# A decoder layer on one core: one comparison per group of tokens against numbers in PSUM, and the gates of a round loaded in quarters

## The chip, the core and the metric

The kernel runs on one core of one Trainium2 chip. The metric is the device time of the whole program in microseconds; the program is launched once per run. TensorE multiplies matrices, VectorE (DVE in the rows), ScalarE (ACT) and GpSimd (POOL) compute element by element, and SyncE (SP) issues most of the DMAs. VectorE and ScalarE read and write both on-chip memories, SBUF and PSUM; in this kernel every GpSimd operand lies in SBUF, and TensorE's results go to PSUM, in eight banks of 512 numbers per partition.

## The reference, cut to what matters

The layer has an input projection, a state-space scan, a windowed attention, an output projection with a layer norm, and then a feed-forward part with 128 x 128 = 16384 experts, of which each token uses 128 (8 heads with 16 each):

```python
e = (jnp.take_along_axis(i1, ci // PEER_TOPK, axis=-1) * PEER_NKEYS
     + jnp.take_along_axis(i2, ci % PEER_TOPK, axis=-1))
g = jax.nn.softmax(sc.astype(F32), axis=-1)
hid = jax.nn.gelu(jnp.einsum('thkd,td->thk', u_tab[e], xb).astype(F32), approximate=False)
return jnp.einsum('thk,thkd->td', (g * hid).astype(xb.dtype), v_tab[e])
```

An expert's number `e` is a row number (0 to 127, `e >> 7`) and a column number (0 to 127, `e & 127`). Only this part is touched by the change.

## The kernel before, in words

There are 1024 prompt tokens and 32 sample tokens. The first 448 prompt tokens have their experts' rows gathered one by one (`gathers`, from line 1808 on: GpSimd issues an indirect DMA for each, VectorE multiplies or accumulates, lines 1855 and 1860). The other 608 tokens go through all 16384 experts as dense products (`dense`, from line 1649 on): hidden values for all experts, times a gate that is zero for experts not chosen, times the second table. The two ways run at the same time: the gathers are a lane that is advanced by ticks between the products' matmuls, at a rate that spreads them over what is left.

**The table of gates.** Before the dense products can use them, the gates must be spread out: for each token a 128 x 128 table, row number by column number, that holds the gate where a chosen expert stands. `gates` builds it for 608 tokens in 152 groups of four. `experts` (line 1549) has put the row numbers (negated, line 1559), column numbers and gates of 128 tokens into a tile `eT` with the chosen experts on the partitions. `build` makes two tiles per group: `o2` (a comparison of 0 to 127 with the column number, line 1603 on VectorE, then times the gate, line 1604 on GpSimd) and `o1` (the same for the row number: on VectorE at line 1610 for three groups of five, on ScalarE at lines 1607 and 1608, as four Abs and one Relu, for two of five). `mults` (line 1617) multiplies them for each token on TensorE, `store` (line 1627) copies the result out of PSUM on ScalarE, and every eighth group goes to DRAM (`gd`, line 1629). `build` runs three groups ahead of `mults`; OBUFS = 4 buffers. One group is done in each tick.

The table is built beside the first six hidden products; `EARLY` gives their numbers of ticks, 8 to 40, so TensorE's order is a piece of a product, then a group's eight passes, and so on. All order is by hand: instructions stand in each engine's queue in the order in which the program issues them.

**The rounds.** The rest of `dense` runs over 16 rounds of eight rows of experts. A round has eight hidden products (Gelu at line 1673 on ScalarE, times the gates at line 1677 on VectorE, split into a high and a low part at lines 1680 and 1683) and eight output products (added to `r` at line 1701), the first two of which are one interleaved pair (`double`, line 1751). Each product is 48 matmuls (line 427). Its weights come in two loads of 256 KB (line 395, SyncE's queue), four products ahead, and are cast into a high part (line 368, ScalarE) and a low part (line 369, mostly GpSimd) two products ahead. Hidden products use three pairs of PSUM banks in turn. The gates of four rows are loaded by `table` (line 1663) as one DMA of 1216 KB from `gd` (line 1670), in pieces of 512 bytes; there are two buffers. The loop calls `table(q + 4)`: the load of a round's first four rows stands beside the fifth output product of the round before, that of the other four beside the round's first hidden product. Ends of groups of gathers (three of 128 tokens and one of 64) run a layer norm in `norm2`, which loads two rows of 512 KB (`lng`, line 1884), multiplies and adds on GpSimd (line 1885) and stores through SyncE's queue (line 1886).

Of the kernel before, what the change touches and what calls it, by code (L numbers as in the profile page):

```python
# [25 lines left out]
NE = 128  # L26
# [27 lines left out]
C_IOTE = C_TSEL + 16  # L54
C_NIOTE = C_IOTE + NE
C_PAY = C_NIOTE + NE
C_N = C_PAY + NPAIR

# [29 lines left out]

EQ, O1, OBUFS, EARLY = 4, "vavav", 4, [8, 16, 24, 30, 34, 40]


def const_arrays():
# [16 lines left out]
    c[:, C_IOTE:C_IOTE + NE] = np.arange(NE)[None, :]  # L109
    c[:, C_NIOTE:C_NIOTE + NE] = -np.arange(NE)[None, :]  # L110
    c[:, C_PAY:C_PAY + NPAIR] = (np.arange(NPAIR)[None, :] + 1) * PACK

# [139 lines left out]
class Build:  # L252
# [40 lines left out]
    def run(self):  # L293
# [10 lines left out]
        self.eps = cp.tile([128, 1], F32, name="eps")  # L304
        self.one = cp.tile([128, 1], F32, name="one")
        self.ctail = cp.tile([128, 20, 3], F32, name="ctail")
# [23 lines left out]
    def start(self):  # L330
        nc, t = self.nc, self.t
        load = [(self.cst, t["cst"]), (self.heads, t["heads"].unsqueeze(0).to_broadcast([128, 2, 24])),
                (self.convw, t["convw"]), (self.chans, t["chans"]), (self.keys, t["keys"])]
        self.xrp = self.open("xr", side="right")
        x = self.inputs(0)
        self.load(0, 0)
        next(x)
        self.load(0, 1)
        next(x)
        self.cast(0, 0)  # L340
        self.load(1, 0)
        next(x)
        self.cast(0, 1)
        self.load(1, 1)
        next(x)
        self.cast(1, 0)
        next(x)
        self.cast(1, 1)
        for _ in x:
            pass  # L350
        self.close("xr")
        for dst, src in load:
            nc.sync.dma_start(dst, src)
        nc.vector.memset(self.eps, EPS)
        nc.vector.memset(self.one, 1.0)
        nc.vector.memset(self.ctail, 0.0)
        nc.scalar.activation(self.heads[:, 1], self.heads[:, 1], AF.Exp)
        nc.vector.tensor_scalar_mul(self.heads[:, 1], self.heads[:, 1], -1.0)

        nc.vector.tensor_scalar_mul(self.convw, self.convw, 0.5)  # L360
        nc.vector.tensor_scalar_mul(self.chans[:, 12:24], self.chans[:, 12:24], 0.5)
# [1187 lines left out]
    def experts(self, sp, table, m, out):  # L1549
# [8 lines left out]
        nc.vector.tensor_copy(en[:m], ej[:m])  # L1558
        nc.vector.tensor_scalar_mul(en[:m, 0], en[:m, 0], -1.0)
        yield  # L1560
# [6 lines left out]
    def gates(self, sp):  # L1567
# [6 lines left out]
        groups = [(w, t) for w in range(len(work)) for t in range(work[w][2], work[w][2] + work[w][0], 4)]  # L1574
        eTs, o12, sts, outs, cp = dict(enumerate(self.given)), {}, {}, {}, {}

        def experts(w):
# [14 lines left out]
        def build(q):  # L1592
# [3 lines left out]
            eT = eTs[w]  # L1596
            o1 = sp.tile([128, 4, 128], F32, name="o1", tag="o1", bufs=OBUFS)
            o2 = sp.tile([128, 4, 128], F32, name="o2", tag="o2", bufs=OBUFS)

            def over(k):  # L1600
                return eT[:, k, t0:t0 + 4].unsqueeze(2).to_broadcast([128, 4, 128])

            nc.vector.tensor_tensor(o2, self.c(C_IOTE).unsqueeze(1).to_broadcast([128, 4, 128]), over(1), op=ALU.is_equal)  # L1603
            nc.gpsimd.tensor_tensor(o2, o2, over(2), op=ALU.mult)  # L1604
            if O1[q % len(O1)] == "a":
                for k in range(4):
                    nc.scalar.activation(o1[:, k], self.c(C_IOTE), AF.Abs, bias=eT[:, 0, t0 + k:t0 + k + 1])
                nc.scalar.activation(o1, o1, AF.Relu, scale=-1.0, bias=self.one)
            else:
                nc.vector.tensor_tensor(o1, self.c(C_NIOTE).unsqueeze(1).to_broadcast([128, 4, 128]), over(0), op=ALU.is_equal)  # L1610
            o12[q] = o1, o2

        def mults(q):
            o1, o2 = o12.pop(q)
            outs[q] = gp = self.bank(q % 3)
            for k in range(4):
                nc.tensor.matmul(gp[:, k * 128:(k + 1) * 128], o2[:, k], o1[:, k], start=True, stop=True)  # L1617

# [30 lines left out]
    def dense(self):  # L1649
# [12 lines left out]

        def table(q):
            if q >= len(steps):
                return
            c, half, k = steps[q]
            if not half and k % 4 == 0:
                gs[c, k // 4] = g = dp.tile([128, n // 32, 4, 32], F32, name="g", tag="g", bufs=2)
                e0 = c * 8 + k
                nc.sync.dma_start(g, self.gd[:, :, e0:e0 + 4, :].rearrange("b j i t -> j b i t"))  # L1670

# [95 lines left out]
        for k in range(8):  # L1767
            if k == len(EARLY):
                self.settle(table_lane)
                self.close("ga", "gc", "best")  # L1770
                dp = self.open("dn", 2)
                for q in range(8):
                    table(q)
            product(4 + k % 2 * 2, hs, EARLY[k] if k < len(EARLY) else DTICKS, lambda ps, k=k: early(k, ps))
# [6 lines left out]
        self.pumping.rate = self.left / ((len(steps) - 8) * DTICKS - 20)  # L1781
        for q in range(8, 12):
            table(q)
        for q, (c, half, k) in enumerate(steps[8:-LASTS], 8):
            table(q + 4)
            if half and k == 0:
# [118 lines left out]
```

## Time and profile before

| what | value |
|---|---|
| median of 3 runs | 3946.99 us (3944.28 to 3955.53) |
| the profiled execution | 3943.13 us, its span 3940.2 us |
| busy: TensorE | 3526.3 us, 89% |
| busy: VectorE | 2826.4 us, 72% |
| busy: GpSimd | 2494.5 us, 63% |
| busy: ScalarE | 1381.6 us, 35% |
| moved by DMA | 875.4 MB, mean 222 GB/s |
| granted clock of TensorE, mean | 0.945 |

How to read it: busy times are sums over the span, and stages with different limits are added up in them. The stretch in which the table of gates is built runs from about 1793 to 2172 us of the span, the rounds from there to about 3890. A line number in a row is that of the program; line 427 is where nearly all products are issued, lines 368, 369 and 395 belong to the weights. "xN" is a count, what stands in brackets or behind "<-" at the end of a row is what ended the idle time in front of it.

### The profile page before, as it was taken

The page shows a single profiled execution, that of the slowest core. Times are in us where ns is not written, and L with a number is a line of the kernel's source. Part 1 is how long each engine was busy: PE and PEld are TensorE (multiplying, and loading weights), DVE is VectorE, ACT ScalarE, POOL GpSimd, SP SyncE. Part 2 cuts the span into 40 slices and gives each one's busy share as a digit, 9 for nine tenths or more (in the row PEclk, how much of TensorE's full clock was granted, in tenths as well). Part 3 has the DMA queues.
Part 4 walks back from the last instruction along what each step waited for, and adds up shares of the span by engine and source line. Part 5 has one row for each costly group of instructions (what it writes and reads, how often), then busy time and mean ns, then how long its engine had stood idle before and what let it go on. Part 6 is the DMA issues. An engine that isn't in the chain of part 4 may idle for free.

```text
span 3940.2 us, 62009 instructions
## 1 busy us (share of the span) xinstructions
PE 3526.3 (89%) x22691; PEld 3178.6 (81%) x22691; DVE 2826.4 (72%) x5547; ACT 1381.6 (35%) x2651; POOL 2494.5 (63%) x2235
## 2 busy tenths in 40 slices
PE   7999898897997887895767999999999999999998
PEld 6757778895765555674666899999999999999997
DVE  2326644488779989899999767667766767776675
ACT  3423324343443333324778222222222222222223
POOL 3204554254747788645788677777767777776774
PEclk9999999998998998897778999999999999999999
DMA  5452235643546457522444789898988999998894
GB/s 159 127 164 74 75 128 199 211 156 107 155 158 212 152 161 249 195 73 78 158 158 185 258 314 324 314 339 316 335 309 318 327 319 339 329 324 304 309 320 154
DMA packets 385521, 875.40 MB, mean 222 GB/s; under 512 B 38976, under 2 KB 149952, under 8 KB 382272
## 3 DMA queue, kind: packets, MB, share of 16 engines
q0 software_dynamic: 129024, 469.82, 33.6%
q1 hardware_dynamic: 256192, 401.63, 30.6%
q8 instruction: 178, 2.92, 0.3%
q14 instruction: 127, 1.04, 0.1%
HBM read 805.40 MB, written 94.65 MB: 228 GB/s over the span
## 4 chain that ended last, share of the span: by engine, by line
PE 38%; DVE 12%; DMA 6%; issue 4%; POOL 3%; ACT 1%; SPq 0%; POOLq 0%; DVEq 0%; ACTq 0%
PE P L427 31%; PE P L1751 5%; DMA wraw<-in_ut 4%; DVE o L1603 2%; DVE acc L1860 2%; DVE o L1610 2%; POOL wlo L369 1%; POOL row L1829 1%; DVE row L1855 1%; POOL o L1604 1%; DMA lng<-in_ln 1%; PE P L1617 1%; DVE mr L1340 0%; PE P L1274 0%; DMA g<-gd 0%
## 5 line engine op out<-in xcount | busy, mean ns | idle before, releaser
L369 POOL TENSOR_TENSOR wlo<-wraw,whi 128x512 fp32r<-128x512 f32 (+1 forms) x621 | 818.2, 1324 | 652.7 <-ACT whi L368 620.5
L368 ACT ACTIVATE whi<-wraw 128x512 fp32r<-128x512 f32 (+1 forms) x820 | 494.8, 625 | 1318.2 <-PE P L427 485.9
L427 PE MATMUL P<-hh,whi 128*128 128x320 f32 (+3 forms) x2648 | 662.5, 315 | 35.9 <-DVE al L1683 27.4
L427 PE MATMUL P<-hh,wlo 128*128 128x320 f32 (+3 forms) x2648 | 655.9, 313 | 17.7 <-DVE wlo L369 9.5
L427 PE MATMUL P<-hl,whi 128*128 128x320 f32 (+3 forms) x2648 | 659.1, 313 | 3.5 <-POOL hl L1295 3.3
L1860 DVE SCALAR_TENSOR_TENSOR P<-row,hid,P 128x1024 f32<-128x1024 f32 x371 | 476.9, 1286 | 57.8 <-DMA row<-in_v,ecol 31.5
L1829 POOL DMA_INDIRECT row<-in_u,ecol x384 | 407.7, 1062 | 152.9 <-DVE row L1855 78.3
L427 PEld LDWEIGHTS P<-hh,whi 128*128 128x128 f32 x2648 | 452.2, 194 | 47.8 <-DVE al L1683 20.8
L427 PEld LDWEIGHTS P<-hh,wlo 128*128 128x128 f32 x2648 | 450.7, 193 | 28.0 <-DVE wlo L369 10.8
L1829 POOL DMA_INDIRECT row<-in_v,ecol x384 | 410.1, 1068 | 90.9 <-issue 71.5
L427 PE MATMUL P<-xh,whi 128*128 128x272 f32 (+4 forms) x1288 | 432.6, 346 | 32.9 <-ACT xh L368 17.3
L427 PEld LDWEIGHTS P<-hl,whi 128*128 128x128 f32 x2648 | 451.5, 193 | 12.8 <-POOL hl L1295 4.7
L1855 DVE SCALAR_TENSOR_TENSOR row<-row,P 128x1024 f32<-128x1024 f32 x320 | 381.8, 1215 | 102.6 <-DMA row<-in_u,ecol 74.0
L427 PE MATMUL P<-xl,whi 128*128 128x272 f32 (+4 forms) x1288 | 420.8, 337 | 7.6 <-POOL xl L369 6.6
L427 PE MATMUL P<-xh,wlo 128*128 128x272 f32 (+4 forms) x1288 | 418.0, 335 | 1.7 <-POOL wlo L369 1.7
L369 DVE TENSOR_TENSOR wlo<-wraw,whi 128x512 fp32r<-128x512 f32 (+1 forms) x199 | 222.7, 1119 | 212.4 <-ACT whi L368 188.3
L427 PE MATMUL P<-ah,wlo 128*128 128x320 f32 (+1 forms) x1536 | 341.9, 302 | 3.1 <-POOL wlo L369 3.1
L427 PE MATMUL P<-ah,whi 128*128 128x320 f32 (+1 forms) x1536 | 342.9, 302 | 0.0
L427 PE MATMUL P<-al,whi 128*128 128x320 f32 (+1 forms) x1536 | 341.4, 301 | 0.0
L1617 PE MATMUL P<-o,o 128*128 128x128 f32 x1216 | 219.2, 338 | 117.1 <-POOL o L1604 99.1
L1617 PEld LDWEIGHTS P<-o,o 128*128 128x128 f32 x1216 | 196.2, 243 | 141.0 <-POOL o L1604 133.6
L427 PEld LDWEIGHTS P<-xh,whi 128*128 128x128 f32 (+1 forms) x1288 | 246.8, 196 | 65.1 <-ACT xh L368 19.1
(393 smaller groups left out, 6794.1 us busy)
## 6 DMA issues: line engine op xcount, KB each, us to landing
wraw<-in_ut SPq DMA_DIRECT2D x256, 256.0 KB
wraw<-in_vd SPq DMA_DIRECT2D x256, 256.0 KB
wraw<-in_wt SPq DMA_DIRECT2D x176, 256.0 KB
gd<-gst SPq DMA_DIRECT2D x19, 2048.0 KB
g<-gd SPq DMA_DIRECT2D x32, 1216.0 KB
wraw<-in_wo SPq DMA_DIRECT2D x64, 256.0 KB
wraw<-in_wq SPq DMA_DIRECT2D x64, 256.0 KB
out_sk<-in_ck SPq DMA_DIRECT2D x8, 2040.0 KB
```

The lines of the kernel that those rows point to most:

```text
L368: nc.scalar.activation(hi, src, AF.Copy)
L369: (eng or nc.vector).tensor_tensor(lo, src, hi.bitcast(F32), op=ALU.subtract)
L427: nc.tensor.matmul(outs[i], w[a][:, k, :m], x[b][k][:, s:s + n], start=first and st, stop=last and sp)
L1603: nc.vector.tensor_tensor(o2, self.c(C_IOTE).unsqueeze(1).to_broadcast([128, 4, 128]), over(1), op=ALU.is_equal)
L1604: nc.gpsimd.tensor_tensor(o2, o2, over(2), op=ALU.mult)
L1610: nc.vector.tensor_tensor(o1, self.c(C_NIOTE).unsqueeze(1).to_broadcast([128, 4, 128]), over(0), op=ALU.is_equal)
L1617: nc.tensor.matmul(gp[:, k * 128:(k + 1) * 128], o2[:, k], o1[:, k], start=True, stop=True)
L1751: nc.tensor.matmul(outs[i][j], self.ws[q0 + i][wi][:, e, :], x[xi][e][:, s:s + m], start=e == p == 0, stop=e == last and p == 2)
L1829: nc.gpsimd.indirect_dma_start(out=rows[k], out_offset=None, in_=t["uv"[tab]], in_offset=bass.IndirectOffsetOnAxis(ap=tables(gi)[0][:, s:s ...
L1855: nc.vector.scalar_tensor_tensor(r, r, 1.0, at, op0=ALU.mult, op1=ALU.mult, accum_out=hid[:, s:s + 1])
L1860: nc.vector.scalar_tensor_tensor(at, r, hid[:, s:s + 1], at, op0=ALU.mult, op1=ALU.add)
```

## The change

In `gates`, the numbers 0 to 127 are copied once to PSUM (bank 3, columns 384 to 511). `build` makes one tile `oo` in place of `o1` and `o2`, by one VectorE comparison of 2 x 4 x 128 elements with row and column numbers at once; the multiplication by the gates on GpSimd stays, in the second half of the tile. ScalarE makes no comparison any more. The row number is no longer negated, and the negated constants and the constant one are gone.

In `dense`, `table` takes a round, a half of its rows and a part. The first two loads are whole as before. In the loop a quarter is loaded beside each output product: the next round's first four rows in quarters beside output products 0 to 3, the other four beside 4 to 7. A quarter is 4 or 5 of the 19 blocks of 32 tokens.

```diff
-        nc.vector.tensor_scalar_mul(en[:m, 0], en[:m, 0], -1.0)
...
+        iota = self.bank(3)[:, 384:]
+        nc.scalar.activation(iota, self.c(C_IOTE), AF.Copy)
...
-            o1 = sp.tile([128, 4, 128], F32, name="o1", tag="o1", bufs=OBUFS)
-            o2 = sp.tile([128, 4, 128], F32, name="o2", tag="o2", bufs=OBUFS)
...
-            nc.vector.tensor_tensor(o2, self.c(C_IOTE).unsqueeze(1).to_broadcast([128, 4, 128]), over(1), op=ALU.is_equal)
-            nc.gpsimd.tensor_tensor(o2, o2, over(2), op=ALU.mult)
-            if O1[q % len(O1)] == "a":
-                for k in range(4):
-                    nc.scalar.activation(o1[:, k], self.c(C_IOTE), AF.Abs, bias=eT[:, 0, t0 + k:t0 + k + 1])
-                nc.scalar.activation(o1, o1, AF.Relu, scale=-1.0, bias=self.one)
-            else:
-                nc.vector.tensor_tensor(o1, self.c(C_NIOTE).unsqueeze(1).to_broadcast([128, 4, 128]), over(0), op=ALU.is_equal)
-            o12[q] = o1, o2
+            oo = sp.tile([128, 2, 4, 128], F32, name="oo", tag="oo", bufs=OBUFS)
+            nc.vector.tensor_tensor(oo, iota.unsqueeze(1).unsqueeze(1).to_broadcast([128, 2, 4, 128]),
+                                    eT[:, 0:2, t0:t0 + 4].unsqueeze(3).to_broadcast([128, 2, 4, 128]), op=ALU.is_equal)
+            nc.gpsimd.tensor_tensor(oo[:, 1], oo[:, 1], eT[:, 2, t0:t0 + 4].unsqueeze(2).to_broadcast([128, 4, 128]), op=ALU.mult)
+            o12[q] = oo
...
-                nc.tensor.matmul(gp[:, k * 128:(k + 1) * 128], o2[:, k], o1[:, k], start=True, stop=True)
+                nc.tensor.matmul(gp[:, k * 128:(k + 1) * 128], oo[:, 1, k], oo[:, 0, k], start=True, stop=True)
...
-        def table(q):
-            if q >= len(steps):
-                return
-            c, half, k = steps[q]
-            if not half and k % 4 == 0:
-                gs[c, k // 4] = g = dp.tile([128, n // 32, 4, 32], F32, name="g", tag="g", bufs=2)
-                e0 = c * 8 + k
-                nc.sync.dma_start(g, self.gd[:, :, e0:e0 + 4, :].rearrange("b j i t -> j b i t"))
+        def table(c, i, part=None):
+
+            if c < NE // 8:
+                if not part:
+                    gs[c, i] = dp.tile([128, n // 32, 4, 32], F32, name="g", tag="g", bufs=2)
+                b, e0 = n // 32, c * 8 + i * 4
+                rows = slice(0, b) if part is None else slice(b * part // 4, b * (part + 1) // 4)
+                nc.sync.dma_start(gs[c, i][:, rows], self.gd[rows, :, e0:e0 + 4, :].rearrange("b j i t -> j b i t"))
...
-                for q in range(8):
-                    table(q)
+                for i in range(2):
+                    table(0, i)
...
-        for q in range(8, 12):
-            table(q)
         for q, (c, half, k) in enumerate(steps[8:-LASTS], 8):
-            table(q + 4)
+            if half:
+
+                table(c + 1, k // 4, k % 4)
```

## Rows read from the trace of the kernel before

**Rows 1.** The page, part 1: busy us, share of the span, instructions of each engine.

```profile
PE 3526.3 (89%) x22691; PEld 3178.6 (81%) x22691; DVE 2826.4 (72%) x5547; ACT 1381.6 (35%) x2651; POOL 2494.5 (63%) x2235
```

**Rows 2.** Stretches: start:end, length, busy us per engine, granted clock, DMA share, GB/s.

```profile
1793.00:2172.00 379.00, 261.98 (x1514) 237.19 (x1515) 373.23 (x480) 269.57 (x472) 305.18 (x212) 0.80 0.41 151
...
2172.00:2310.00 138.00, 125.68 (x863) 122.87 (x862) 103.70 (x93) 37.42 (x63) 94.86 (x80) 0.96 0.82 284
...
2538.50:2645.50 107.00, 107.00 (x771) 107.00 (x770) 76.72 (x125) 28.81 (x49) 83.47 (x78) 1.00 0.95 343
...
3515.40:3636.30 120.90, 112.34 (x771) 111.85 (x769) 80.27 (x107) 33.02 (x54) 85.40 (x77) 0.94 0.90 310
```

**Rows 3.** Instruction groups in 1793 to 2172: xcount, busy us, mean ns, idle before.

```profile
L1617 PE MATMUL P<-o,o 128*128 128x128 f32 x1216 | 219.2, 338 | 117.1 <-POOL o L1604 99.1 <-DVE o L1610 8.9 <-ACT gst L1627 8.0
...
L1604 POOL TENSOR_TENSOR o<-o,eT 128x512 f32<-128x512 f32 x152 | 210.6, 1395 | 88.1 <-DVE o L1603 85.3 <-DVE ei L1546 2.4
...
L1603 DVE TENSOR_TENSOR o<-cst,eT 128x512 f32<-128x512 f32 x152 | 151.6, 1019 | 0.8 <-ACT eT L1565 0.8
...
L1610 DVE TENSOR_TENSOR o<-cst,eT 128x512 f32<-128x512 f32 x91 | 105.5, 1160 | 0.0
...
L1607 ACT ACTIVATE o<-cst,eT 128x128 f32<-128x128 f32 x236 | 73.4, 390 | 0.0
...
L1608 ACT ACTIVATE o<-o,one 128x512 f32<-128x512 f32 x59 | 42.6, 722 | 1.9
...
L1860 DVE SCALAR_TENSOR_TENSOR acc<-row,hid,acc 128x1024 f32<-128x1024 f32 x31 | 67.2, 2167 | 0.0
```

**Rows 4.** Lines 1603 and 1604 alone: count, shortest/median/longest ns, first and last start.

```profile
L1603 DVE TENSOR_TENSOR o<-cst,eT x152: 674/680/2847, 1793.0 to 2165.5; 128x512 f32<-128x512 f32 x152
...
L1604 POOL TENSOR_TENSOR o<-o,eT x152: 1032/1421/3162, 1793.8 to 2167.1; 128x512 f32<-128x512 f32 x152
```

**Rows 5.** Lines 1855, 1860, 1683 alone, whole span: VectorE with and without PSUM operand.

```profile
L1855 DVE SCALAR_TENSOR_TENSOR row<-row,P x320: 1200/1216/1224, 2337.9 to 3726.9; 128x1024 f32<-128x1024 f32 x160
...
L1860 DVE SCALAR_TENSOR_TENSOR P<-row,hid,P x371: 1273/1289/1292, 2212.7 to 3873.0; 128x1024 f32<-128x1024 f32 x186
...
L1860 DVE SCALAR_TENSOR_TENSOR acc<-row,hid,acc x77: 1270/2056/3393, 1535.8 to 2207.8; 128x1024 f32<-128x1024 f32 x77
...
L1683 DVE TENSOR_TENSOR al<-P,ah x120: 775/785/794, 2267.4 to 3859.4; 128x608 fp32r<-128x608 f32 x120
```

**Rows 6.** The chain of waits in order of time: start, us, step.

```profile
2310.11 13.37 PE P L1751 x96
...
2376.99 17.70 DMA wraw<-in_ut
...
2399.68 29.06 PE P L427 x192
...
3855.20 13.38 PE P L1751 x96
```

**Rows 7.** In order of time, 2640 to 2760, SyncE's queue and ScalarE: start, us, instruction.

```profile
2700.53 0.43 SPq L1670 DMA_DIRECT2D g<-gd  x1
...
2689.57 0.63 ACT L368 ACTIVATE whi<-wraw 128x512 fp32r<-128x512 f32 x1 [9.74 <-DMA wraw<-in_ut]
...
2691.38 0.64 ACT L368 ACTIVATE whi<-wraw 128x512 fp32r<-128x512 f32 x1 [1.18 <-DMA wraw<-in_ut]
...
2721.37 0.63 ACT L368 ACTIVATE whi<-wraw 128x512 fp32r<-128x512 f32 x1 [12.69 <-DMA wraw<-in_ut]
```

**Rows 8.** Who TensorE waited for, 2172 to 3855: us, times, longest.

```profile
PE P L427 <- DVE al L1683: 27.4, 8, 6.1
...
PE P L427 <- POOL wlo L369: 8.4, 4, 4.7
```

**Rows 9.** Who SyncE's queue waited for, 2310 to 3890: us, times, longest.

```profile
SPq L395 <- DMA wraw<-in_ut: 205.1, 29, 10.2
...
SPq L1886 <- POOL acc L1885: 31.4, 3, 11.3
```

More of the change, by code (lines that the diff above doesn't have):

```diff
@@ L54 @@
 C_IOTE = C_TSEL + 16
-C_NIOTE = C_IOTE + NE
-C_PAY = C_NIOTE + NE
+C_PAY = C_IOTE + NE
 C_N = C_PAY + NPAIR
@@ L86 @@
 NLO = "vpvpvpvp"
-EQ, O1, OBUFS, EARLY = 4, "vavav", 4, [8, 16, 24, 30, 34, 40]
+EQ, OBUFS, EARLY = 4, 4, [8, 16, 24, 30, 34, 40]
 def const_arrays():
@@ L109, in const_arrays @@
     c[:, C_IOTE:C_IOTE + NE] = np.arange(NE)[None, :]
-    c[:, C_NIOTE:C_NIOTE + NE] = -np.arange(NE)[None, :]
     c[:, C_PAY:C_PAY + NPAIR] = (np.arange(NPAIR)[None, :] + 1) * PACK
@@ L304, in run @@
         self.eps = cp.tile([128, 1], F32, name="eps")
-        self.one = cp.tile([128, 1], F32, name="one")
         self.ctail = cp.tile([128, 20, 3], F32, name="ctail")
@@ L354, in start @@
         nc.vector.memset(self.eps, EPS)
-        nc.vector.memset(self.one, 1.0)
         nc.vector.memset(self.ctail, 0.0)
@@ L1596, in build @@
             eT = eTs[w]
-            o1 = sp.tile([128, 4, 128], F32, name="o1", tag="o1", bufs=OBUFS)
-            o2 = sp.tile([128, 4, 128], F32, name="o2", tag="o2", bufs=OBUFS)
-            def over(k):
-                return eT[:, k, t0:t0 + 4].unsqueeze(2).to_broadcast([128, 4, 128])
-            nc.vector.tensor_tensor(o2, self.c(C_IOTE).unsqueeze(1).to_broadcast([128, 4, 128]), over(1), op=ALU.is_equal)
-            nc.gpsimd.tensor_tensor(o2, o2, over(2), op=ALU.mult)
-            if O1[q % len(O1)] == "a":
-                for k in range(4):
-                    nc.scalar.activation(o1[:, k], self.c(C_IOTE), AF.Abs, bias=eT[:, 0, t0 + k:t0 + k + 1])
-                nc.scalar.activation(o1, o1, AF.Relu, scale=-1.0, bias=self.one)
-            else:
-                nc.vector.tensor_tensor(o1, self.c(C_NIOTE).unsqueeze(1).to_broadcast([128, 4, 128]), over(0), op=ALU.is_equal)
-            o12[q] = o1, o2
+            oo = sp.tile([128, 2, 4, 128], F32, name="oo", tag="oo", bufs=OBUFS)
[3 more added lines that the diff above has]
+            o12[q] = oo
         def mults(q):
-            o1, o2 = o12.pop(q)
+            oo = o12.pop(q)
             outs[q] = gp = self.bank(q % 3)
             for k in range(4):
-                nc.tensor.matmul(gp[:, k * 128:(k + 1) * 128], o2[:, k], o1[:, k], start=True, stop=True)
+                nc.tensor.matmul(gp[:, k * 128:(k + 1) * 128], oo[:, 1, k], oo[:, 0, k], start=True, stop=True)
         def store(q):
```

## The prediction

> **What bounds the kernel now.** The busy line comes first [rows 1]: TensorE works 89% of the span, no other engine over 72%. A mean over stages cannot price either edit, so the table of stretches is next [rows 2]. The stretch 1793 to 2172 is the one in which the gates' table is built; there TensorE is busy 262.0 of 379 us at a granted clock of 0.80 (between its two levels of 1.2 and 2.4 GHz), while VectorE is busy 373.2 of 379. So VectorE bounds this stretch. The stretch 2538.5 to 2645.5 is one round over eight experts' rows: TensorE busy 107.0 of 107.0 at clock 1.00. That is a floor which neither edit touches. The stretch 3515.4 to 3636.3 is the same work in 120.9 us, so some rounds are disturbed. Third, the instruction groups of the table stretch, to see what VectorE does there [rows 3], and the spread of single durations [rows 4, 5]. Last, the chain of waits, the order in time of one clean round, and who waited for whom [rows 6 to 9], for the rounds.
>
> **The change part by part. First edit: one comparison against numbers in PSUM.** Before, each of the 152 groups of four tokens takes one VectorE comparison for o2 (151.6 us in all) and, for 91 of them, a second for o1 (105.5): 257.1 us of VectorE [rows 3]. The other 61 go to ScalarE. After, each group is one VectorE comparison over 1024 elements, 152 in all, and ScalarE makes none.
>
> What does it cost? Line 1603, 512 elements and both operands in SBUF, has a shortest and a median of 674 and 680 ns, but a mean of 1019 and a longest of 2847 [rows 3, 4]; on GpSimd the multiplication beside it goes from 1032 to a median of 1421 [rows 4]. So both engines lose when both read SBUF. The accumulation of line 1860 shows it on VectorE best: with its operands in SBUF it takes 1270 to 3393 ns, and 2167 in the mean in this stretch; the same operation with one operand in PSUM takes 1273 to 1292 in all 371 cases, although GpSimd is busy some three quarters of that time (83.5 of 107 us) [rows 2, 3, 5]. Line 1683 has the very pattern of the new operation (one operand PSUM, one SBUF, result SBUF): 775 to 794 ns for 608 elements in 120 cases [rows 5]. The trace has no comparison of 1024 elements with a PSUM operand. Its bounds are 1.20 us (the shortest of line 1855, 1024 elements, one PSUM operand, result in SBUF) and 2.17 us (line 1860 with SBUF operands in this stretch). I take 1.22, the median of line 1855, which it resembles most. 152 x 1.22 = 185 us, so VectorE is relieved of 257 - 185 = 72 us.
>
> VectorE's other work in the stretch is 373.2 - 257.1 = 116 us. 67.2 of it are 31 accumulations at 2.17 us whose operands stay in SBUF; uncontended they would be 39. GpSimd's multiplication still reads SBUF, so I give back only about 10 of these 28 us; the smaller removed negation is under 3 us. VectorE's new sum is 185 + 116 - 11 = 290 us.
>
> What is late next? TensorE was busy 262 at clock 0.80 and would have to fit into the shorter stretch; GpSimd 305, of which 211 is the multiplication, at 1.40 us each against 1.03 alone [rows 2 to 4]: 152 x 1.1 + 95 = 262. ScalarE falls from 270 by 73.4 + 42.6 = 116 us; it was not the limit, so this earns nothing directly. The one copy of the numbers into PSUM is about the size of line 1607, 0.39 us, and stands once in front of the first comparison; the next wait in line is then the first matmul group, behind nothing else. With three engines near 262 to 290, VectorE cannot keep its 98.5%; I take 94%: 290 / 0.94 = 308 us, against 379: **71 us saved**. Ends: 275 us if the contention goes entirely (104 saved), 340 if TensorE at the lower clock becomes the limit (39 saved); with the dearer end of the comparison this part loses, see the rivals. The stores of the table and the gathers of the stretch keep their place in the order of ticks; the DMA share there is only 0.41, so a shorter stretch has room.
>
> **Second edit: the gates of a round in quarters.** Before, two loads of 1216 KB per round, one beside the fifth output product, one beside the first hidden product. After, eight loads of a quarter each, one beside each of the eight output products. Bytes are equal; SyncE issues eight times instead of two, at 0.43 us each [rows 7]: 2.6 us more per round, in a queue whose long waits are for buffers. The first two loads, ahead of the rounds, are unchanged. No new wait arises for the buffers: the first table's is read for the last time in hidden product 3 and its first quarter is issued four products later; the second's in hidden product 7, its first quarter also four later. The multiplication by the gates now waits for four landings, the last some four products (27 us) ahead of use.
>
> What does a whole load do now? In a clean round it is issued at 2700.53, and the weights queued behind it reach ScalarE only at 2721.37, after ScalarE stood 12.7 us; weights with no such load in front follow 1.8 us apart (2689.57, 2691.38) [rows 7]. So a whole load holds the queue about 19 us. SyncE shows the same: 29 waits, 205 us, on weights' DMA, where 14 rounds with two whole loads each make 28 [rows 9]. In the hidden half ScalarE's queue holds the Gelus behind that cast, so the PSUM pairs come free late: TensorE's waits for line 1683 are 27.4 us in 8 places [rows 8], and the chain runs over such a load (17.7 us at 2376.99) into the restart at 2399.68 [rows 6]. Clean rounds absorb it; disturbed ones do not. From 2310.11 to 3855.20 are 14 rounds: 1545.1 - 14 x 107.0 = 47 us over the floor [rows 2, 6]. A stall costs more than its idle time, since the clock falls: 120.9 - 107.0 = 13.9 us for 120.9 - 112.3 = 8.6 idle [rows 2]. After, no load of gates stands in the hidden half. I leave one of the eight waits to the ends of the groups of gathers and count seven eighths of the 27.4 us, 24, as lying behind such loads; times 1.25, between idling without a fall of the clock (1.0) and 13.9 / 8.6, gives **30 us saved**. The rest stays: at the end of a group of gathers SyncE waits for GpSimd (31.4 us in 3 places [rows 9]), which quarters do not shorten. Ends: 45 saved (all of the excess), and a loss, next paragraph.
>
> The price of quarters is not in the trace. In the output half the queue must now move 8 quarters (2 x 19 = 38 us at the measured pace) and 16 loads of weights (16 x 1.8 = 29): 67 us in a half of 53.5. So weights can be up to 13.5 us late at the end of it, and the hidden half, with 29 us of loads, takes this up. Clean rounds already stand 12.7 us without TensorE idling, so I count nothing for it, but the margin is thin: that is a rival. From the other side, a large load and its weights overlap with gathers that stop meanwhile, so the 19 us are no lower end. The Trainium skill speaks against this edit: "DMA: Bandwidth & Descriptors", section Bandwidth, says to batch transfers to at least 1 MiB, with 78% of peak at 1 MB (6.15 us) and 32% at 64 KB (0.95 us). Interpolated, an estimate from that page, a quarter would take some 2.25 us and four of them 9.0 against 7.2 for the whole, 3.6 us per round; if it all reached TensorE, that is 50 us in 14 rounds, and the sum would be 3896. The trace bears this out little: 256 KB loads followed each other at 1.8 us.
>
> **The sum.** The profiled execution took 3943.1 us (span 3940.2, 2.9 around it), 3.9 below the median of 3947.0. 3943.1 - 71 - 30 = 3842; plus 3.9 for the median: **3846 us**. The likeliest case's own range is 3815 to 3868.
>
> **The rivals.** (1) Another engine takes the bound: the table stretch stops at 340 us because TensorE, pausing for each group, stays at the lower clock. For it: clock 0.80 and 117 us of idle time in its groups [rows 2, 3]; against: 99 of those 117 wait for GpSimd, which waits for VectorE [rows 3]. 3947 - 39 - 30 = 3878. (2) The quarters do nothing: the hold-ups come from the gathers and from SyncE's wait at their ends, or the weights come as late as before, in smaller portions. For it: DMA share 0.95 in a clean round [rows 2]. 3947 - 71 = 3876. (3) The quarters cost: the output half is overloaded and each of 14 rounds loses about 4 us (the sum of two 13.5 us delays missing their cover, spread): 3947 - 71 + 56 = 3932 at worst, 3904 in the middle. The rule on batches, cited above from the Trainium skill, belongs to this case. (4) Slower: the comparison contends although its numbers lie in PSUM, because the gates' side and the result are in SBUF. At 2.17 us, 152 of them are 330 us, 73 more than now, and GpSimd gains nothing; with the 30 of the rounds 3947 + 73 - 30 = 3990. The edit decides against itself from 257.1 / 152 = 1.69 us per comparison. Against it: lines 1683 and 1860 in PSUM, 491 cases without one long one [rows 5].
>
> **How the numbers follow.** Forecast 0.58; (1) 0.14; (2) 0.13; (3) 0.08; (4) 0.04; and 0.03 that gains and losses cancel. For eight in ten the range takes in most of the first, and (1) and (2): 3812 to 3895. Within 0.3%, about what a measurement can tell here, is 3935 to 3959: 0.03. Slower: 0.04. Faster: 0.93.
>
> **What would show it.** Right: the comparison at 1.20 to 1.25 us with hardly any spread; GpSimd's multiplication near 1.1; the stretch near 308 us with VectorE below 98%; no TensorE wait for line 1683's successor in rounds without the end of a group of gathers; ScalarE's waits for weights under 8 us. Wrong: comparisons of two lengths as now; TensorE's clock below 0.8 in the stretch with waits for its own results; in the rounds, idle TensorE in the output half, or late weights in the first hidden products of rounds that were clean.

## The result and the profile after

The changed kernel takes 3836.8 us (median of 4 runs, 3831.2 to 3837.8) against 3945.6 in the runs beside it: ratio 0.972, 95% interval 0.9695 to 0.9746. The forecast was 3846, its range 3812 to 3895. The profiled execution took 3836.0 us, its span is 3834.2, 106.0 less than before.

The page's busy line, for [rows 1]:

```profile
PE 3486.9 (91%) x22691; PEld 3149.7 (82%) x22691; DVE 2737.8 (71%) x5449; ACT 1286.0 (34%) x2347; POOL 2449.3 (64%) x2235
```

The stretches, for [rows 2], in the same columns: the table's stretch, the first piece of a round behind it, a disturbed round, a clean one, another disturbed one:

```profile
1792.00:2104.50 312.50, 227.44 (x1518) 210.18 (x1519) 290.83 (x387) 173.68 (x177) 257.28 (x212) 0.87 0.50 183
2104.50:2236.90 132.40, 124.68 (x860) 122.46 (x859) 106.37 (x94) 37.98 (x63) 97.95 (x82) 0.96 0.87 306
2236.90:2349.20 112.30, 108.91 (x770) 108.66 (x770) 78.34 (x114) 33.32 (x54) 82.92 (x75) 0.98 0.91 323
2349.20:2456.40 107.20, 107.20 (x769) 107.20 (x769) 76.76 (x122) 28.56 (x49) 80.92 (x75) 1.00 0.96 335
...
3421.60:3536.00 114.40, 110.00 (x770) 109.75 (x769) 80.20 (x106) 33.41 (x54) 85.51 (x77) 0.97 0.93 323
```

The table's stretch is 66.5 us shorter between these bounds. VectorE is no longer busy in 98% but in 93% of it, and the granted clock is 0.87 instead of 0.80, nearer to the upper of its two levels. The instruction groups in it, for [rows 3], in the same columns, and the two lines alone, for [rows 4]:

```profile
L1606 PE MATMUL P<-oo 128*128 128x128 f32 x1216 | 192.3, 309 | 86.5 <-POOL oo L1599 86.3
L1599 POOL TENSOR_TENSOR oo<-oo,eT 128x512 f32<-128x512 f32 x152 | 182.7, 1216 | 68.8 <-DVE oo L1597 65.6 <-DVE ei L1542 0.5
L1597 DVE TENSOR_TENSOR oo<-P,eT 128x1024 f32<-128x1024 f32 x152 | 177.8, 1211 | 7.2 <-ACT eT L1560 3.0 <-PE P L1558 2.1 <-PE P L1606 2.0
...
L1849 DVE SCALAR_TENSOR_TENSOR acc<-row,hid,acc 128x1024 f32<-128x1024 f32 x31 | 57.2, 1844 | 0.0
...
L1597 DVE TENSOR_TENSOR oo<-P,eT x152: 1202/1210/1226, 1792.4 to 2097.6; 128x1024 f32<-128x1024 f32 x152
...
L1599 POOL TENSOR_TENSOR oo<-oo,eT x152: 1028/1041/2034, 1793.7 to 2099.6; 128x512 f32<-128x512 f32 x152
```

Line 1597 is the joined comparison: 152 times nearly the same length. The rest of the gain is in the rounds. The chain of waits in order of time, for [rows 6]: the end of the table (its last store to `gd`), where rounds begin (line 1740 is the interleaved pair), and what lies in the first, disturbed one:

```profile
2104.79 6.24 DMA gd<-gst
...
2236.90 13.37 PE P L1740 x96
...
2255.10 6.97 DMA row<-in_u,ecol
2262.07 10.18 DMA lng<-in_ln
...
2280.98 68.22 PE P L423 x476
2349.20 13.39 PE P L1740 x96
2362.59 93.85 PE P L423 x672
2456.44 13.37 PE P L1740 x96
...
3421.61 13.37 PE P L1740 x96
...
3750.52 13.39 PE P L1740 x96
```

The same chain before the change, the end of its table and two clean rounds:

```profile
2172.40 6.24 DMA gd<-gst
...
2538.50 13.37 PE P L1751 x96
...
2645.45 13.37 PE P L1751 x96
```

Fourteen rounds now take 3750.52 - 2236.90 = 1513.6 us, 31.5 less than before. No piece of the chain in the rounds is a transfer of weights any more in this execution; what remains is the end of a group of gathers, the loads of line 1873 (`lng`) and what follows them on GpSimd. The longest waits of TensorE (2090 to 3770) and of SyncE's queue (2230 to 3770), for [rows 8, 9]:

```profile
PE P L423 <- POOL wlo L365: 7.8, 2, 4.4
PE P L1740 <- ACT ah L1669: 6.4, 1, 6.4
...
PE P L1740 <- DVE al L1672: 0.2, 1, 0.2
...
SPq L1875 <- POOL acc L1874: 34.9, 3, 14.2
SPq L391 <- DMA wraw<-in_ut: 29.7, 20, 3.6
SPq L391 <- DMA wraw<-in_vd: 13.1, 6, 4.8
```

SyncE's 205 us behind weights' DMA are 43: 30 for the weights of hidden products (`in_ut`), and 13 for those of output products (`in_vd`), for which it did not wait before. And the 27.4 us that TensorE waited for the low part of the hidden values are gone. The 106.0 us split into 67.6 up to the end of the table (2104.8 instead of 2172.4), 5.6 for the piece behind it (137.7 to 132.1), 31.5 for fourteen rounds and 1.3 for the tail.

One loss is among it: a clean round takes 107.24 us (2349.20 to 2456.44) where it took 106.95 (2538.50 to 2645.45), with no idle time in either. Fourteen rounds lose about 4 us by it.

### The profile page after: what moved, and what is told of

It reads as the page before. It is cut to its first block, busy times and chain, and to the rows that moved or that the text cites. A ratio compares the mean times of both kernels' runs of the same rounds, so it can differ in the third digit from the quotient of the medians.

```text
span 3834.2 us, 61736 instructions
## 1 busy us (share of the span) xinstructions
PE 3486.9 (91%) x22691; PEld 3149.7 (82%) x22691; DVE 2737.8 (71%) x5449; ACT 1286.0 (34%) x2347; POOL 2449.3 (64%) x2235
## 3 DMA queue, kind: packets, MB, share of 16 engines
q1 hardware_dynamic: 257632, 401.57, 31.5%
## 4 chain that ended last, share of the span: by engine, by line
PE 46%; DVE 8%; POOL 4%; issue 3%; DMA 2%; ACT 0%; DVEq 0%; POOLq 0%; ACTq 0%; SPq 0%
PE P L423 39%; PE P L1740 5%; DVE oo L1597 2%; POOL oo L1599 1%; PE P L1606 1%; DVE acc L1849 1%; POOL row L1818 1%; DVE mr L1336 1%; POOL eq L1537 0%; POOL wlo L365 0%; DMA row<-in_v,ecol 0%; DVE keys L1340 0%; DVE keys L1334 0%; DVE row L1844 0%; DMA g<-gd 0%
## 5 line engine op out<-in xcount | busy, mean ns | idle before, releaser
L1849 DVE SCALAR_TENSOR_TENSOR P<-row,hid,P 128x1024 f32<-128x1024 f32 x371 | 476.6, 1285 | 23.8 <-DMA row<-in_v,ecol 13.5
L1818 POOL DMA_INDIRECT row<-in_v,ecol x384 | 394.3, 1027 | 104.5 <-issue 50.3
L365 DVE TENSOR_TENSOR wlo<-wraw,whi 128x512 fp32r<-128x512 f32 (+1 forms) x199 | 203.5, 1023 | 205.6 <-ACT whi L364 195.8
L423 PEld LDWEIGHTS P<-xl,whi 128*128 128x128 f32 (+1 forms) x1288 | 246.7, 196 | 35.1 <-POOL xl L365 9.7
L1606 PE MATMUL P<-oo 128*128 128x128 f32 x1216 | 192.3, 309 | 86.5 <-POOL oo L1599 86.3
```

The costliest lines, as they stand in the source:

```text
L365: (eng or nc.vector).tensor_tensor(lo, src, hi.bitcast(F32), op=ALU.subtract)
L423: nc.tensor.matmul(outs[i], w[a][:, k, :m], x[b][k][:, s:s + n], start=first and st, stop=last and sp)
L1606: nc.tensor.matmul(gp[:, k * 128:(k + 1) * 128], oo[:, 1, k], oo[:, 0, k], start=True, stop=True)
L1818: nc.gpsimd.indirect_dma_start(out=rows[k], out_offset=None, in_=t["uv"[tab]], in_offset=bass.IndirectOffsetOnAxis(ap=tables(gi)[0][:, s:s ...
L1849: nc.vector.scalar_tensor_tensor(at, r, hid[:, s:s + 1], at, op0=ALU.mult, op1=ALU.add)
```

## Experiments

All medians of before that stand beside the runs lie at 3943 to 3950 us. Single runs of it go from 3934 to 3961, so parts are added up by the spans of the profiled executions.

### Each edit alone

The first edit alone (comparison and PSUM, loads of the gates as before):

```diff
-        def table(c, i, part=None):
+        def table(q):
...
-                table(c + 1, k // 4, k % 4)
+            table(q + 4)
```

> The gates' edit alone; the gates of a round are loaded whole as before. If the two edits act in different stretches and simply add up, the table stretch is 312 us as in the changed kernel, the 14 rounds take about 1545 us as before (47 us over 14 clean rounds), and the time is about 3946 - 68 = 3878 us (ratio 0.983). Rival: the gain in the rounds came from the earlier start or from another position of the gathers, not from the quarters; then the rounds shorten here too and the time is near 3845.

Measured: 3879.7 us, ratio 0.9835 (0.9804 to 0.9865), span 3877.4. The second edit alone, the new `table` in the kernel before:

```diff
-        def table(q):
+        def table(c, i, part=None):
...
-            table(q + 4)
+            if half:
+                table(c + 1, k // 4, k % 4)
```

> The quarters alone; the table is built as before. If the edits add up: table stretch 379 us, 14 rounds about 1514 us, time about 3946 - 37 = 3909 us (ratio 0.991). Rival (the quarters do little by themselves): 3940 or more.

Measured: 3896.9 us, ratio 0.9868 (0.984 to 0.9896), span 3899.8. The spans are 62.8 and 40.4 us shorter than before's, together 103.2 of the 106.0: within what these runs can tell the edits add up and neither needs the other. (By the medians they are 1.65% and 1.32%, together 2.97% against 2.79%; the intervals are too wide to tell these apart.) Waits of the first edit alone, TensorE's from 2100 and SyncE's from 2230 on, to 3800:

```profile
PE P L423 <- DVE al L1672: 23.3, 11, 4.5
...
SPq L391 <- DMA wraw<-in_ut: 212.3, 29, 11.1
```

These are before's waits. So the second edit removed them, not the shorter table. The rounds themselves are 10.2 us longer than before's in thirteen (1443.3 against 1433.1 by the chain), some 4 of it by the longer clean rounds. The second edit was worth more than was forecast: 30.7 us in thirteen rounds (1433.1 to 1402.5), where the forecast had 30 in fourteen, and the rounds begin 5.6 us earlier (2304.50 instead of 2310.11), which the forecast left out.

### The numbers in SBUF: the disputed cost by itself

```diff
-        iota = self.bank(3)[:, 384:]
-        nc.scalar.activation(iota, self.c(C_IOTE), AF.Copy)
+        iota = self.c(C_IOTE)
```

> The changed kernel with the numbers 0 to 127 read from SBUF instead of PSUM; everything else is as in the changed kernel, one joined comparison per group. Theory (VectorE and GpSimd hinder each other when both read two SBUF operands, and PSUM avoids it): the comparison is no longer uniform; its mean rises from 1.21 to 1.7 to 2.2 us, GpSimd's multiplication to about 1.4; VectorE gets 75 to 150 us more to do in the table stretch, which becomes 370 to 440 us, and the time 3900 to 3965. Rival (joining two comparisons into one was the gain, and taking ScalarE's part away): the comparison stays near 1.25 us and the time within 10 us of the changed kernel's 3837.

Measured: 3923.9 us, ratio 0.9941 (0.9922 to 0.996), 87 more than the changed kernel. The table's stretch, the two lines (shortest/median/longest), and the comparison as a group (busy, mean):

```profile
1790.00:2191.00 401.00, 271.74 (x1507) 244.09 (x1508) 385.27 (x387) 173.59 (x176) 353.47 (x212) 0.77 0.39 142
...
L1596 DVE TENSOR_TENSOR oo<-cst,eT x152: 1202/2055/3718, 1790.2 to 2185.8; 128x1024 f32<-128x1024 f32 x152
...
L1598 POOL TENSOR_TENSOR oo<-oo,eT x152: 1030/2016/3024, 1791.6 to 2187.9; 128x512 f32<-128x512 f32 x152
...
L1596 DVE TENSOR_TENSOR oo<-cst,eT 128x1024 f32<-128x1024 f32 x152 | 268.3, 1805 | 4.0 <-PE P L1605 3.7 <-ACT eT L1560 0.3
```

Same comparisons, same elements; only where one operand lies differs. The shortest durations are unchanged, the medians are 0.85 us longer on VectorE and 0.98 longer on GpSimd, and the stretch is 401 us, 22 longer than before the change. The join, which also takes over ScalarE's share, would have lost in this stretch; the PSUM operand brings more than the whole of the first edit's gain there. This is the cost that rival (4) feared, made real by other means: at 1.805 us in the mean the edit loses there, as the prediction's bound of 1.69 us said it would.

The Trainium skill, "SBUF — State Buffer", section "SBUF: two separate sides", says that a VectorE operation with two SBUF inputs takes a port pair against a GpSimd operation that reads SBUF, and that the loser waits until the other is through. The rows fit that: the medians, 2.06 and 2.02, come within a tenth of the sum of the two alone (1.21 + 1.03 = 2.24), and with one input in PSUM line 1597 never exceeds 1.226 us. They do not show a lock as such.

### Two comparisons in place of the joined one

```diff
-            nc.vector.tensor_tensor(oo, iota..., eT[:, 0:2, t0:t0 + 4]..., op=ALU.is_equal)
+            for k in (1, 0):
+                nc.vector.tensor_tensor(oo[:, k], iota..., eT[:, k, t0:t0 + 4]..., op=ALU.is_equal)
```

> The changed kernel with two comparisons of 512 elements per group, both on VectorE and both against the numbers in PSUM. Theory: each takes about 0.69 us without spread, 1.38 per group against 1.21, so VectorE has 26 us more to do; with VectorE at 93 to 97% the table stretch is 330 to 340 us and the time 3855 to 3865. Rival (VectorE no longer bounds the stretch, the chain VectorE, GpSimd, TensorE of each group does): time unchanged within 6 us, since the column's comparison stands first and GpSimd gets its operand earlier.

Measured: 3838.0 us, ratio 0.9723 (0.9695 to 0.975): no difference from the joined one. Stretch and comparison:

```profile
1793.60:2106.00 312.40, 229.77 (x1521) 214.24 (x1522) 300.22 (x537) 173.37 (x178) 251.37 (x212) 0.85 0.50 182
...
L1598 DVE TENSOR_TENSOR oo<-P,eT x304: 670/674/692, 1793.6 to 2102.1; 128x512 f32<-128x512 f32 x152
```

VectorE is busy 9.4 us more (one by one the comparisons add up to 21 us more, 304 x 0.674 against 152 x 1.210), and the stretch is as long as the changed kernel's. So joining brought nothing, and VectorE had room for 9 us: in the changed kernel it no longer sets the stretch alone. One thing is not separated here: the comparison that GpSimd waits for comes first, so GpSimd gets its operand earlier, which may have made up for VectorE's 9 us.

### Two groups of five on ScalarE again

```diff
+            if q % 5 in (1, 3):
+                nc.vector.tensor_tensor(oo[:, 1], iota..., eT[:, 1, t0:t0 + 4]..., op=ALU.is_equal)
+                for k in range(4):
+                    nc.scalar.activation(oo[:, 0, k], self.c(C_IOTE), AF.Abs, scale=-1.0, bias=eT[:, 0, t0 + k:t0 + k + 1])
+                nc.scalar.activation(oo[:, 0], oo[:, 0], AF.Relu, scale=-1.0, bias=self.c(C_ONE, 1))
+            else:
...
```

> The changed kernel with the row's comparison of two groups in five given back to ScalarE (four Abs and one Relu, as before), the column's staying on VectorE against PSUM; the other groups keep the joined comparison. VectorE has some 30 us less of 178 to do in the table stretch, ScalarE 116 more (174 to 290 of about 312). Theory (VectorE still binds, at 93%): the stretch becomes 290 to 305 us, time 3815 to 3830. Rivals: the chain of each group through VectorE, GpSimd and TensorE binds: no change within 5 us; or relieving ScalarE was part of the gain: the stretch becomes longer than 312 us, time 3845 to 3870.

Measured: 3834.1 us, ratio 0.9717 (0.9701 to 0.9733), again no difference in the time. The stretch, and TensorE's two longest waits in it (1840 to 2100):

```profile
1792.00:2104.00 312.00, 223.72 (x1534) 205.04 (x1535) 265.50 (x396) 264.99 (x474) 255.07 (x213) 0.90 0.51 185
...
PE P L1613 <- POOL oo L1606: 41.2, 36, 3.1
PE P L1613 <- ACT gst L1623: 29.2, 26, 2.4
```

VectorE has 25 us less to do, and between these bounds the stretch is 0.5 us shorter. TensorE's waits for GpSimd fall from 64.1 us in 51 places to 41.2, and 29.2 us of waits for ScalarE's copies out of PSUM take their place. The bounds are round numbers; sharper is the time from the table's first matmul to the start of its last. In the changed kernel, and in the kernel of the last experiment below, which gives one group of five to ScalarE (VectorE 274.6 us in its stretch), it reads:

```profile
L1606 PE MATMUL P<-oo x1216: 270/275/583, 1794.8 to 2103.3; 128*128 128x128 f32 x174
...
L1615 PE MATMUL P<-oo x1216: 270/275/582, 1793.9 to 2094.4; 128*128 128x128 f32 x174
```

That is 308.5 and 300.5 us, and 304.6 with two groups of five. All other kernels with the first edit and the PSUM operand lie at 307.6 to 308.9, the one with 300 us of VectorE among them. So relieving VectorE by 16 and 25 us shortens the table by 8 and 4 us, one profiled execution each: the table follows VectorE only in part. The changed kernel's chain of waits through the stretch goes 23.6% over the comparison, 17.0% over GpSimd's multiplication and 14.4% over the matmuls, where before the two comparisons on VectorE had 40.5%. So several engines that hand each group on in a fixed order through four buffers would explain the rest; more buffers weren't tried, so what sets it stays open.

### Place and size of the loads, one at a time

Whole loads in the output half (beside output products 0 and 4):

```diff
-                table(c + 1, k // 4, k % 4)
+                if k % 4 == 0:
+                    table(c + 1, k // 4)
```

> The changed kernel, but the gates of a round are loaded whole: four rows beside output product 0, the other four beside output product 4, so both loads stand in the output half as the quarters do, only uncut. Theory (the place decides: no load of gates in front of the weights in the half in which ScalarE's queue also holds the Gelus): most of the gain in the rounds stays, 14 rounds in at most 1525 us (changed kernel 1514, before 1545), time 3837 to 3850. Rival (the cutting decides, since a whole load holds the weights for 19 us wherever it stands): 14 rounds near 1545, time near 3870.

Measured: 3847.5 us, ratio 0.9763 (0.9742 to 0.9783). Quarters at the old places, four in a row:

```diff
-            if half:
-                table(c + 1, k // 4, k % 4)
+            at = (c + 1, 0) if half and k == 4 else (c, 1) if not half and k == 0 else None
+            if at:
+                for part in range(4):
+                    table(*at, part)
```

> The changed kernel, but the quarters stand four at once at the two old places: beside output product 4 and beside the first hidden product. Theory (the place decides): TensorE's waits for line 1672 come back in disturbed rounds, 14 rounds near 1540 us, time 3865 to 3880. Rival (cutting alone lets the weights in between): the four quarters land in pieces, 14 rounds near 1515, time near 3840.

Measured: 3871.1 us, ratio 0.9821 (0.9802 to 0.984). And no loads in the rounds: every round multiplies by the first round's gates, so it leaves out the loads and the layer's values are others:

```diff
-            if half:
-                table(c + 1, k // 4, k % 4)
+            for i in range(2):
+                gs[c + 1, i] = gs[0, i]
```

> The changed kernel without any load of gates in the rounds: every round multiplies by the gates of the first round, so the numbers that come out are not the layer's; the rest of the work is the same. It gives the floor for any way of loading gates. Theory (the quarters are fully hidden, the rest of the excess comes from the ends of the groups of gathers): 14 rounds within 5 us of the changed kernel's 1514, time 3830 to 3840. Rival (the quarters still cost, as DMA time that the gathers and weights lack): the two disturbed rounds (112.3 and 114.4 us) become clean, 14 rounds near 1502, time near 3822.

Measured: 3824.8 us, ratio 0.9691 (0.9663 to 0.9719). The five kernels with the first edit side by side; thirteen rounds by the chain, less 13 clean rounds of 107.25 us:

| loads of the gates | 13 rounds, us | over 13 clean ones | span, us |
|---|---|---|---|
| whole, old places (first edit alone) | 1443.3 | 49.1 | 3877.4 |
| quarters, old places | 1432.3 | 38.0 | 3867.8 |
| whole, output half (from the first piece shown, 2233.55) | 1418.5 | 24.3 | 3843.2 |
| quarters, output half (the changed kernel) | 1406.4 | 12.1 | 3834.2 |
| none | 1396.8 | 2.6 | 3824.4 |

The place gives 25 to 26 us, at either size; cutting gives 11 to 12, at either place; what is left of the loads costs some 10. In medians the cut at the old places isn't resolved (0.9821 against 0.9835, with intervals that overlap), in the output half it is hardly so (0.9763 against 0.9721), so the 11 to 12 rest on the records, one profiled execution each; the whole spans differ by 9.6 and 9.0. SyncE's waits of 2230 to 3770, whole loads in the output half:

```profile
SPq L391 <- DMA wraw<-in_ut: 104.5, 16, 9.5
...
SPq L391 <- DMA wraw<-in_vd: 26.6, 10, 6.0
```

and quarters at the old places, with TensorE's wait:

```profile
SPq L391 <- DMA wraw<-in_ut: 197.4, 29, 10.5
...
PE P L423 <- DVE al L1672: 19.0, 8, 5.1
```

Where a whole load stands, weights are late behind it, and four quarters in a row hold the queue about as long as a whole. In the hidden half that reached TensorE: the quarters at the old places still leave it 19.0 us of waits for line 1672 (the low part of the hidden values) in 8 places. With whole loads in the output half it has none there.

What the quarters still cost, they cost in the rounds with the end of a group of gathers. The first round and a clean one without loads:

```profile
2345.40:2452.64 107.24, 107.24 (x771) 107.24 (x770) 74.31 (x120) 28.27 (x49) 79.78 (x74) 1.00 0.89 306
2236.75:2345.40 108.65, 107.51 (x770) 107.26 (x770) 78.95 (x115) 33.43 (x54) 83.89 (x76) 1.00 0.88 318
```

The clean round is 107.24 with or without loads: eight quarters in an output half cost nothing there. The first round is 108.65 instead of 112.30, and the clock does not fall in it.

### The 0.3 us of a clean round

Rival causes were the loads of the gates (excluded by the row above: 107.24 without them) and the place of the tiles in SBUF. The tiles laid out behind the removed constants lie lower than before, by 512 bytes for the negated constants and by 32 for the constant one. An unused tile of 4 bytes takes back the 32:

```diff
+        self.one = cp.tile([128, 1], F32, name="one")
...
+        nc.vector.memset(self.one, 1.0)
```

> The changed kernel with the constant tile of 4 bytes that the change removed put back, unused. It moves all later tiles in SBUF by 32 bytes. In the changed kernel a clean round takes 107.25 us against 106.95 before and with the quarters alone, so something in the first edit costs 0.3 us per round in the hidden half. If the position of the tiles does it, clean rounds are 106.95 us here, and the span is about 4 to 5 us shorter; if not, 107.25 and no change.

Measured: 3831.1 us, ratio 0.971 (0.9694 to 0.9726). Chain of waits, clean rounds:

```profile
2356.73 13.38 PE P L1742 x96
2463.65 13.37 PE P L1742 x96
2570.60 13.38 PE P L1742 x96
2677.52 13.37 PE P L1742 x96
```

Rounds of 106.92, 106.95 and 106.92 us, as before the change. Every kernel here without the constant tile has clean rounds of 107.2 to 107.3 us, every one with it 106.9 to 107.0. The place of the tiles is shown as the cause; which tile it is, and why it matters to TensorE, is not. The span, 3836.5, doesn't show it: thirteen rounds take 4.9 us less than the changed kernel's (1401.5 against 1406.4), but they begin 6.4 us later (2243.26 instead of 2236.90). The median is 5.7 us lower, and its interval overlaps the changed kernel's.

### Towards a better version

The unused tile, and line 1875's store issued from GpSimd's queue, so that SyncE no longer waits for GpSimd there:

```diff
-        nc.sync.dma_start(dst, acc)
+        nc.gpsimd.dma_start(dst, acc)
```

> The changed kernel with the unused constant tile put back (clean rounds of 106.95 us) and with the result of a group of gathers stored from GpSimd's queue in place of SyncE's, so that SyncE no longer waits for GpSimd (34.9 us in 3 places) with weights queued behind that wait. If this wait is what disturbs the rounds at the ends of groups, the disturbed rounds lose less (12 us over the floor in 14 rounds becomes 0 to 6), and the time is 3822 to 3832. Rival (GpSimd's own stop, for the two rows of the norm and the two operations on them, holds the casts): only the 5 us of the tile, 3830 to 3835.

Measured: 3831.5 us, ratio 0.9715 (0.969 to 0.9741). The same with one group of five on ScalarE (`q % 5 in (2,)` in the edit above):

> As the kernel with the tile put back and the store on GpSimd's queue, and one group in five has its row's comparison on ScalarE. With two in five the stretch kept its 312 us, with VectorE at 265 and ScalarE at 265, and TensorE then waited 29 us for ScalarE's copies. If the two loads trade off, one in five (VectorE some 278, ScalarE some 220) gives 302 to 310 us, so 2 to 10 us under the kernel without it. If a chain of all engines binds instead, no difference over 3 us.

Measured: 3832.2 us, ratio 0.971 (0.9685 to 0.9735). Neither stands out from the changed kernel's 0.972. The shorter table of the second, shown above, is not seen in its time: its five runs go from 3825 to 3835. The chain of the first of the two over its first round (2220 to 2360):

```profile
2251.08 6.98 DMA row<-in_u,ecol
2258.06 10.48 DMA lng<-in_ln
...
2268.68 2.40 POOL acc L1876
...
2271.15 2.40 POOL acc L1876
...
2346.40 13.37 PE P L1742 x96
```

SyncE's 34.9 us of waits are gone, and the round still takes 113.5 us (2232.91 to 2346.40). Thirteen rounds lie 14.9 us over clean ones of 106.95; with the unused tile alone it was 11.2. So that wait was idle time which cost nothing. GpSimd itself stands for the two rows of `lng`, then works 4.8 us at line 1876, and the low parts of the weights (line 367), which it also makes, stand behind that in its queue.

## Why the prediction was right

The result lies inside the range and 9 us below the forecast. By its steps:

- **The comparison, 1.22 us:** 1.210, from 1.202 to 1.226. Right, and by the reason given: with the numbers in SBUF its median is 2.055. Line 1855, the nearest in shape, was the right row to take.
- **VectorE's new sum, 290 us:** 290.8. Its parts were right within 8 us, and the two misses cancel: the comparisons 177.8 busy (185), all else 113.0 (105), with the accumulations at 57.2 (67.2 less 10, so 57).
- **GpSimd, 262 us with a multiplication of 1.1:** 257.3, by luck. The median is 1.041 but the mean 1.216: most run as if alone, some still last up to 2.034, as if they met VectorE's operations on SBUF. So the multiplications take 182.7 us where 167 stood, and the rest of GpSimd's work 75 where 95 stood.
- **The stretch, 308 us at 94% of VectorE:** 312.5 at 93%, so 67 us saved where 71 stood. The size was right, the reason only in part. VectorE's 290 us were taken as what the stretch hangs on; with 300 it is just as long, with 265 and 275 only 4 and 8 us shorter. The 94% was a chosen allowance for the other engines and not worked out from a row. Rival (1) did not occur: the clock rose to 0.87, and of TensorE's 86.5 us of waits at the table's matmuls 86.3 are for GpSimd. Its 340 us had no row behind it either.
- **The quarters, 30 us:** 31.5 in the fourteen rounds. Two things are missing in it: the 5.6 us of the piece ahead, and 4 us that the longer clean rounds took back (the prediction held a clean round for a floor that neither edit touches). The excess over clean rounds fell by more than was forecast, from 47.8 to 1513.6 - 14 x 107.25 = 12.1.
- **What a whole load does:** right in the mechanism. But the prediction did not separate place from size: of some 37 us in thirteen rounds, 25 are the place and 12 the cutting.
- **An output half overloaded by 13.5 us:** not seen. With eight quarters a clean round shows no idle TensorE (107.20 of 107.20). ScalarE's waits for weights are at most 7.9 us between the two disturbed rounds, and there are none in the clean one from 2456 to 2564. The step added 38 us of loads to 29 us of weights as if they went one after the other. In the output half from 2456 on, the eight quarters take 7.6 to 11.5 us each from issue to landing, 9.2 in the median; that is 74 us in a half of 53.5, so they overlap. Rival (3) falls. Rival (2), quarters that do nothing, stood at 3876; the first edit alone, which is that case, measured 3879.7, so this rival was priced rightly and did not occur. Rival (4) was priced too high: 2.17 us for a comparison and 3990 in all, where the run with the numbers in SBUF has 1.805 in the mean and 3923.9.
- **The rule on batches** ("DMA: Bandwidth & Descriptors", section Bandwidth, of the Trainium skill), by which the time would have been 3896: not borne out here. Quarters beat whole loads at both places in the records. The page's figures are of loads issued from GpSimd, and the gates' are issued from SyncE. The 1.8 us that the prediction set against the rule said little: the same interpolation, again an estimate from that page, gives some 2.0 us for 256 KB.
- **ScalarE's waits for weights under 8 us:** wrong. The longest is 15.3 us, in the second disturbed round; outside the two disturbed rounds it is 7.9. Without any loads of gates it is still 11.1, in the first round, so most of it belongs to the ends of the gathers and was wrongly laid to the loads.
- **The ends of the groups of gathers stay:** right as a time (34.9 us of SyncE's waits, 31.4 before), wrong in the place. SyncE's wait was named; the run without it gains nothing in those rounds. And of the 47 us over clean rounds the prediction left some 17 to these ends as out of reach of the loads. With no loads of gates only 2.6 us are left in thirteen rounds, though the ends are still there: an end by itself costs next to nothing, an end together with loads does.
- **The sum:** 101 us off the profiled execution's 3943.1, and 3.9 for its distance to the median. The profiled times differ by 107.2, and the new one lies 0.9 under its median instead of 3.9: 6.2 + 3.0 = 9.2 us.

## What to carry to other kernels

When two engines take turns on SBUF, read the shortest duration and the median of an operation side by side: a median far over the shortest was the sign of contention here, and one operand moved to PSUM may be worth more than fewer instructions. A large load on the queue that also brings the weights should stand where late weights don't reach the busiest engine, as in the output half here, and cutting it then helps a little more. Once an engine is relieved, don't count on it as the bound: a second run with more or less work on it shows whether the stretch still follows.

## What the runs showed of the hardware that was not expected

Moving most tiles by 32 bytes in SBUF changed a clean round of 768 matmuls without idle time from 106.95 to 107.24 us, 0.3%; the unused tile of 4 bytes brought it back. And a VectorE comparison of 512 elements costs 0.674 us with one operand in PSUM, as against 0.674 at the shortest with both in SBUF [rows 4]: the PSUM operand itself costs nothing here; what it saves is the time that the two engines lost to each other.
